# Contracting the second pass of the context logits over 104 rows in place of 64

## The chip, the cores and the metric

The kernel runs on one core of a Trainium2 chip. The metric is the device time of one execution in microseconds. Three timed runs of the kernel before gave 1978.53, 1979.91 and 1981.23 us; their median, 1979.91 us, is the time to be compared with.

## The reference

A network of four layers works on 1024 tokens (a grid of 16 rows and 64 columns) of 1024 features, with 256 further context tokens. Each layer norms its input, scales and shifts it, applies a mixer and adds the result to the stream. The mixers are pooling, neighbourhood attention, short convolution, and pooling again. The change lies in the attention, layer 1, which has 16 heads of 64 features. Each query sees keys in a window of the grid, with a bias, and all 256 context keys:

```python
s_ctx = jnp.einsum('brqhd,bchd->bhrqc', q, kc).astype(jnp.float32)
logits = jnp.concatenate([s_loc.reshape(...), s_ctx], axis=-1)
p = jax.nn.softmax(logits, axis=-1).astype(v.dtype)
```

All is float32.

## The kernel before

Activations lie transposed, features on partitions. A float32 value is held as two parts, hi + lo, each of which TensorE takes in one pass, and a product is hi*hi + hi*lo + lo*hi. The large projections do this in three matmuls per feature tile (`mm3`, L115 to L117).

In the attention (`na_attend`) the tokens stand in 8 blocks of 8 grid columns, 128 queries each, so there are 16 heads x 8 blocks = 128 steps. A head has 64 features, which is half of the 128 rows that a matmul can contract over. The logits use this: the first pass contracts over 128 rows, with the query's hi and lo part stacked (64 + 64) against the key's hi part twice. The second pass has the query's hi part (64 rows) against the key's lo part (64 rows). For the keys of the grid the second pass carries 40 more rows (`MROWS`): one-hot rows of the query's place against rows of 0 or -1e30 that mask the window. So for the grid's keys (PSUM tile `S`) it contracts over `KK` = 64 + 40 = 104 rows (L1153), and for the 256 context keys (tile `SC`), which need no mask, over 64 (L1155). In all four products the queries are the loaded weights and the keys are streamed.

One step of the loop is, in TensorE's order: for every second step the values of a pair of blocks (`O`, L1234 and L1235, alternately with the hi and the lo part of the probabilities); the transposes of one block's probabilities (`T`, and `TB` for a fifth chunk, L1209); about two and a half items of dense work (the projections of the next heads, later a share of the output projection); and the four products of the logits of the block three steps ahead (L1152 to L1155). Between them VectorE takes the maximum of the logits (L1167 for `SC`, L1169 for `S`), ScalarE the exponential (L1179), GpSimd multiplies by the reciprocal of the sum (`normalise`, L1188), and after the transposes ScalarE and VectorE split the result in hi and lo (`pthi` L1213, `ptlo` L1218). `S`, `SC`, `O` and `TB` have one buffer each, `T` has two.

The order on each engine is the order in which the program is written, and each engine runs its own in turn. `load_keys` issues the loads of a head's keys and values, one head ahead, on SyncE's queue. GpSimd's other work in this stretch is the lo part of weights (`wlo`, L80) and a gating product per pair of heads (L1244).

Of the kernel before, what the change touches and what calls it, by code (L numbers as in the profile page):

```python
"""Hybrid pool / neighbourhood-attention / short-conv backbone on one core.

Activations live transposed: features on partitions, tokens along the free axis.  A float32
product x*w is carried by three passes of the tensor engine over exact parts: x = xh + xl,
w = wh + wl (each part fits the engine's single-pass operand), xh*wh + xl*wh + xh*wl.
"""
# [10 lines left out]
F32 = mybir.dt.float32  # L17
# [7 lines left out]
P = 128  # L25
# [16 lines left out]
# columns of the packed per-feature vectors  # L42
# [4 lines left out]
class Tiles(list):  # L47
    """feature tiles of a chunk of tokens, and the pairs of them that share a slot"""
# [5 lines left out]
class Net:  # L54
# [8 lines left out]
    # ---------------------------------------------------------------- storage  # L63
# [6 lines left out]
    # chunks of tokens: halves, the two parts of the second half, the context  # L70
# [5 lines left out]
    # ---------------------------------------------------------------- pieces  # L76
    def split(self, hi, lo, src, lo_engine=None):
        """src (float32) = hi + lo"""
        self.nc.scalar.activation(hi, src, AF.Copy)  # L79
        (lo_engine or self.nc.vector).tensor_tensor(lo, src, hi.bitcast(F32), op=ALU.subtract)  # L80
# [15 lines left out]
    def weight_later(self, src, c0=0, c1=1024, lo_engine=None):  # L96
        """a weight whose parts are split by the steps that come with it"""
        raw = self.pw.tile([P, 1024], F32, tag="raw", name=self.nm("raw"), bufs=3)
        self.nc.sync.dma_start(raw[:, c0:c1], src[:, c0:c1])
        hi = self.pw.tile([P, 1024], F32R, tag="whi", name=self.nm("whi"))  # L100
        lo = self.pw.tile([P, 1024], F32R, tag="wlo", name=self.nm("wlo"))

        def step(c):
            s = slice(c, min(c + 256, c1))
            self.split(hi[:, s], lo[:, s], raw[:, s], lo_engine)
        return (hi, lo), [lambda c=c: step(c) for c in range(c0, c1, 256)]

    def mm3(self, ps, w, h, ks, begin=True, end=True):
        """ps (+)= sum over ks of w(k)^T h(k), both operands as pairs of parts"""
        t = self.nc.tensor  # L110
        ks = list(ks)
        for k in ks:
            wh, wl = w(k)
            hh, hl = h(k)
            t.matmul(ps, wh, hh, start=(begin and k == ks[0]), stop=False)  # L115
            t.matmul(ps, wh, hl, start=False, stop=False)  # L116
            t.matmul(ps, wl, hh, start=False, stop=(end and k == ks[-1]))  # L117

    def ahead(self, fetch, args):
        """fetch(*a) for a in args, one ahead of its use"""  # L120
# [20 lines left out]
    # Short dependent products are traced a few long ones after their operands, so that the  # L141
    # tensor engine, which runs in this order, does not wait for them.
# [13 lines left out]
    # ---------------------------------------------------------------- modulation  # L156
    def ada_tile(self, l, conds, j, raw=None):
        """column j (128 features) of silu(cond) @ ada_w[l] + ada_b[l]"""
# [11 lines left out]
    def gain(self, l, c, k0=0, k1=KT):  # L170
        """A = norm_g * (1 + scale)"""
# [5 lines left out]
    def ada_all(self, l, x_parts, c_parts=()):  # L177
        """the modulation of a layer, one tile at a time"""
# [12 lines left out]
    def background(self, n=None):  # L191
        """modulation of later layers, between the weights of this one"""
# [15 lines left out]
    # ---------------------------------------------------------------- rms norm  # L208
# [7 lines left out]
    def sumsq_add(self, st, x, k, engine=None, whole=True):  # L216
        """the squares are summed here, the last one optionally by the product that sums partitions"""
# [12 lines left out]
    def rstd_tokens(self, st):  # L230
        """1/sqrt(mean square + eps), tokens on partitions"""
# [42 lines left out]
    def rstd_spread(self, dg, n):  # L274
        """the same on all partitions, tokens along the free axis (PSUM)"""
# [5 lines left out]
    def norm_later(self, xs, st, l, c, n, h, key, delays=(1, 2)):  # L281
        """h[key] = parts of the modulated norm of xs, traced behind the next products"""
# [16 lines left out]
    def modulate_k(self, x, rs, l, c, k, hi, lo, n, pool=None, act=False):  # L299
        """(hi, lo) parts of x * rstd * A + B for one feature tile"""  # L300
# [12 lines left out]
    def hparts(self, n=HALF):  # L313
        """fresh (hi, lo) tiles for the 8 feature tiles of one chunk of tokens"""
# [26 lines left out]
    # ---------------------------------------------------------------- out projection  # L341
    def out_proj(self, wsrc, y, l, groups, xold, spill, order=range(KT), ks={}):
        """x_new[k] (per chunk) = xold + gate * (y @ w_out); sums of squares on the way.  The chunks of a
        group share their weights.  `ks` may
        restrict the sum of a chunk's tile to some feature tiles, with the others' share in xold."""
# [31 lines left out]
    # ---------------------------------------------------------------- pooling mixer  # L377
    POOL_ORDER = (6, 7, 4, 5, 2, 3, 0, 1)

    def pool_in(self, li, h, chunks, start=None):  # L380
        """y (float32) per feature tile: {k: {ch: AP}}; `start` may make the first products itself"""
# [6 lines left out]
        def put(t, ch, ps=None):  # L388
# [19 lines left out]
            if ch == "c":  # L408
                dst = y[k][ch] if kind == "g" else Uc[k][:, 16:16 + CTX]
                # the products of the shifts  # L410
# [22 lines left out]
        def mix(gi, ch, Wg):  # L433
# [12 lines left out]
            for j, k in enumerate(ks):  # L446
                u = Uc[k] if ch == "c" else U[k]
                # sum over the window [t - w/2, t + w/2) by doubling
# [10 lines left out]
                # windows cut by an end of the sequence hold fewer tokens  # L459
# [21 lines left out]
        # products that do not wait for the second half of the tokens come first  # L481
# [20 lines left out]
        for t in todo:  # L502
# [9 lines left out]
            # the mixing products of the group before, now that their operands are there  # L512
# [11 lines left out]
    # ---------------------------------------------------------------- layers  # L524
# [28 lines left out]
    def consts(self):  # L553
# [12 lines left out]
        # the conditions on all partitions  # L566
# [8 lines left out]
        # per layer and kind of token: gain, (shift, scale, gate)  # L575
# [6 lines left out]
    def squares(self, x):  # L582
        """sum of the squares of a half's tokens, but for the sum over partitions"""
# [14 lines left out]
    def load_pair(self, xs, src, k, off):  # L598
        """feature tiles k and k + 1, which share a slot"""
# [3 lines left out]
    def scratch(self):  # L603
# [5 lines left out]
        # keys of pairs, values of fours of heads  # L609
# [15 lines left out]
    def layer0(self):  # L625
# [7 lines left out]
        # out tokens by halves of the grid's columns  # L633
# [16 lines left out]
    def start(self, h, put, shift, W):  # L650
        """the norms of layer 0 and the first products.  A half's products are those of x * A, as the
        modulation of each feature tile arrives; 1/rms of the tokens and the products of the shift,
        which go along with the context's as one more token, come to them afterwards."""
# [19 lines left out]
        def block(t):  # L673
            """the weights of a tile, which lie in blocks of P columns ordered by k, then tile"""
# [7 lines left out]
        # the order in which the operands are needed  # L682
# [11 lines left out]
        def high(ch, x, k):  # L694
            """(hi, lo) parts of x * A"""
# [31 lines left out]
        def square(ch, x, j):  # L727
            """the squares of a pair of tiles are summed"""
# [73 lines left out]
        def gained_c(k):  # L802
            """the same for the context, the shifts of both kinds of tokens as two more tokens"""
# [78 lines left out]
    # ---------------------------------------------------------------- neighbourhood attention  # L882
    def store_kq(self, part, hp, ch, ps):
        """parts of a pair's keys or scaled queries to DRAM"""
# [21 lines left out]
    def kq_steps(self, pairs, h, early=None):  # L906
        """the projections of pairs' keys and queries, a few matrix products at a time; `early`
        is stepped along once the last pair is done with the first half of the tokens"""
# [34 lines left out]
    def mask_rows(self):  # L943
        """constant rows of the attention operands, rounded to their type"""
# [8 lines left out]
    def na_first(self, h):  # L953
        """values and gates of all heads, keys and queries of the first pair"""
# [51 lines left out]
    def y_rows(self, y, p):  # L1006
        """parts of half p of the grid's rows, from tokens in column-block order"""
# [11 lines left out]
    def x1_rows(self, ch, k):  # L1019
        """half of the rows of the residual, from tokens in column-block order"""  # L1020
# [8 lines left out]
    def out_ahead(self):  # L1029
        """operands of out_steps"""  # L1030
# [17 lines left out]
    def out_steps(self):  # L1048
        """the first heads' share of the output's first half (and of a little more), while the
        last heads attend"""  # L1050
# [28 lines left out]
    def load_keys(self, h):  # L1079
# [11 lines left out]
        ld(KC[0:HD, CTX:2 * CTX], self.dkc[hp][1, r])  # L1091
        dv = self.dv[h // 4][:, :, h % 4]
# [13 lines left out]
    def na_attend(self, hx):  # L1106
        """returns y (float32, tokens in column-block order) per feature tile"""
# [26 lines left out]
        def logits(n):  # L1134
# [20 lines left out]
            nc.tensor.matmul(SC[:], Q[0:HD, 1, q0], KC[0:HD, CTX:2 * CTX], start=False, stop=True)  # L1155
            tiles[n] = (S, SC)

        def maximum(n):
# [6 lines left out]
            # negated logits and their minimum  # L1165
# [24 lines left out]
        def transpose(n):  # L1190
# [4 lines left out]
            # chunk order: key blocks up to 2mp+1, context, then (odd b) block 2mp+2  # L1195
# [54 lines left out]
        # stores are issued once their data are there, so that the loads behind them do not wait  # L1250
# [151 lines left out]
def _edges():  # L1402
    e = np.ones((P, 4, 16), np.float32)
    for gi in range(4):
# [3 lines left out]
        for j in range(w // 2 - 1):  # L1408
            # tokens L - (w/2 - 1) + j
# [29 lines left out]
def _ntiles(w, cols=P):  # L1439
    """[K, N] -> [N/cols, 128, K/128 * cols]: per tile of output features, contiguous per partition"""  # L1440
# [4 lines left out]
def _interleave(w, tiles):  # L1445
    """chosen tiles of _ntiles, their blocks of P columns ordered by k, then tile"""
# [4 lines left out]
def _feat(a):  # L1451
    """[..., F] -> [128, ... * F/128]"""
# [4 lines left out]
def _blocks(xT):  # L1457
    """row-major grid tokens -> column blocks of 8"""
# [4 lines left out]
def _bias(rpb):  # L1463
    """[16, 15, 31] -> [16, 128 queries (r, c), 3 * 128 keys (block offset, r', c')], zero outside the table"""
# [48 lines left out]
```

## Time and profile before

| what | value |
|---|---|
| timed runs, median (lowest to highest) | 1979.91 us (1978.53 to 1981.23) |
| span of the profiled execution | 1977.3 us |
| device time of that execution | not listed apart from its span |
| PE (matmul) busy | 1902.4 us, 96% |
| PEld (weight load) busy | 1607.0 us, 81% |
| DVE, ACT, POOL busy | 1103.4, 727.7, 565.1 us |
| chain that ended last, by engine | PE 77%, DVE 12%, DMA 5% |
| chain, by line: L1155 | 2% |

PE is TensorE's matmuls and PEld its weight loads, which can run beside a matmul. DVE is VectorE, ACT ScalarE, POOL GpSimd and SPq the queue of SyncE, which issues the DMAs. The spans of matmuls are modelled at their ends, and matmuls overlap in the pipeline: how fast TensorE goes through them is read from the distance of their starts, not from their lengths.

### The profile page before, as it was taken

To read this page: it belongs to the slowest core of one execution; us is meant where nothing else is said; L and a number is where in the kernel's file an instruction comes from. 1 tells how busy PE (TensorE), PEld (TensorE's weight loads), DVE (VectorE), ACT (ScalarE), POOL (GpSimd) and SP (SyncE) were. 2 spreads that over 40 slices of the span, in tenths; PEclk is the share of its full clock that TensorE was granted. 3 is DMA by queue.
4 is the path that set the end of the run, shared out by engine and by line. 5 is a ranking of instruction groups with operands and counts; after the bars stand their busy time and mean duration, and the time that the engine had idled before them with its cause. 6 is when DMAs were issued, how large, how long until landed. Compare 5 with 4: busy or idle time off the path is not lost.

```text
span 1977.3 us, 27078 instructions
## 1 busy us (share of the span) xinstructions
PE 1902.4 (96%) x9936; PEld 1607.0 (81%) x9936; DVE 1103.4 (56%) x2251; ACT 727.7 (37%) x1401; POOL 565.1 (29%) x536
## 2 busy tenths in 40 slices
PE   7789889999999999999999999999999999999997
PEld 4677778889988888888887787788888887888887
DVE  7989986346521066666666668744222246532536
ACT  3432225344122255555555656321122135322322
POOL 4545323552110133333333434100000023333120
PEclk9899999999999999999999999999999999999999
DMA  6232362554863456566568637534111155011234
GB/s 248 75 112 91 116 193 59 192 165 136 277 200 107 157 160 180 178 191 180 159 185 233 194 107 232 173 113 132 45 52 48 48 181 171 16 49 48 67 123 152
DMA packets 126960, 274.21 MB, mean 139 GB/s; under 512 B 12874, under 2 KB 48458, under 8 KB 126828
## 3 DMA queue, kind: packets, MB, share of 16 engines
q1 hardware_dynamic: 126828, 272.49, 44.3%
q8 instruction: 78, 1.28, 0.3%
q14 instruction: 54, 0.44, 0.1%
HBM read 218.63 MB, written 53.81 MB: 138 GB/s over the span
## 4 chain that ended last, share of the span: by engine, by line
PE 77%; DVE 12%; DMA 5%; issue 3%; POOL 2%; ACT 1%; SPq 0%; DVEq 0%; POOLq 0%; ACTq 0%
PE mm L115 21%; PE mm L117 21%; PE mm L116 21%; DVE junk L166 4%; PE T L1209 3%; PE O L1234 3%; PE O L1235 2%; PE SC L1155 2%; DMA raw<-in_ada 2%; PE S L1152 1%; DMA a<-x 1%; PE S L1153 1%; DVE S L455 1%; POOL S L455 1%; DMA a<-in_xT 1%
## 5 line engine op out<-in xcount | busy, mean ns | idle before, releaser
L115 PE MATMUL mm<-a,whi 128*128 128x512 f32 (+2 forms) x2160 | 820.2, 380 | 23.5 <-DVE U L418 11.1
L117 PE MATMUL mm<-a,wlo 128*128 128x512 f32 (+2 forms) x2160 | 806.5, 373 | 5.0 <-POOL wlo L80 3.3
L116 PE MATMUL mm<-a,whi 128*128 128x512 f32 (+2 forms) x2149 | 802.8, 374 | 7.4 <-DVE a L80 6.6
L115 PEld LDWEIGHTS mm<-a,whi 128*128 128x128 f32 x2160 | 410.6, 190 | 95.6 <-DVE U L418 12.4
L117 PEld LDWEIGHTS mm<-a,wlo 128*128 128x128 f32 x2160 | 409.6, 190 | 79.7 <-POOL wlo L80 4.8
L116 PEld LDWEIGHTS mm<-a,whi 128*128 128x128 f32 x2149 | 408.7, 190 | 76.6 <-DVE a L80 8.4
L79 ACT ACTIVATE whi<-raw 128x1024 fp32r<-128x1024 f32 (+2 forms) x237 | 170.8, 738 | 356.2 <-PE mm L116 273.3
L80 POOL TENSOR_TENSOR wlo<-raw,whi 128x256 fp32r<-128x256 f32 (+2 forms) x150 | 190.0, 1280 | 386.8 <-ACT whi L79 359.8
L1188 POOL TENSOR_SCALAR pr<-pr,rsum 128x640 f32<-128x640 f32 (+1 forms) x128 | 99.1, 774 | 277.3 <-DVE rsum L1187 252.5
L166 DVE CUSTOM_DVE_ANT_0 junk<-raw,sil_x,vec 128x1024 bf16<-128x1024 f32 x86 | 120.3, 1399 | 91.7 <-DMA raw<-in_ada 91.4
L80 DVE TENSOR_TENSOR wlo<-raw,whi 128x1024 fp32r<-128x1024 f32 (+1 forms) x87 | 108.1, 1243 | 112.2 <-ACT whi L79 111.2
L115 PE MATMUL mm<-a,a 128*128 128x512 f32 (+2 forms) x280 | 98.0, 350 | 8.6 <-ACT a L698 7.4
L1167 DVE TENSOR_SCALAR_CACHE_REDUCE lg<-SC 128x256 f32<-128x256 f32 x128 | 54.3, 424 | 92.8 <-PE SC L1155 92.3
L1179 ACT ACTIVATE pr<-lg,nmx 128x640 f32<-128x640 f32 (+1 forms) x128 | 102.2, 799 | 1.9 <-DVE nmx L1169 1.9
L224 POOL TENSOR_TENSOR a<-a,a 128x512 f32<-128x512 f32 x42 | 59.9, 1427 | 142.0 <-ACT a L223 133.2
L116 PE MATMUL mm<-a,a 128*128 128x512 f32 (+2 forms) x275 | 96.1, 350 | 3.8 <-DVE a L702 3.0
L117 PE MATMUL mm<-a,a 128*128 128x512 f32 (+2 forms) x280 | 97.0, 346 | 0.5 <-DVE a L80 0.5
L1218 DVE TENSOR_TENSOR ptlo<-T,pthi 128x512 fp32r<-128x512 f32 x128 | 88.5, 692 | 14.8 <-ACT pthi L1213 10.9
L1234 PE MATMUL O<-pthi,a 128*128 128x256 f32 x352 | 93.5, 301 | 1.1 <-ACT pthi L1213 1.1
L1235 PE MATMUL O<-ptlo,a 128*128 128x256 f32 x352 | 87.4, 284 | 0.6 <-DVE ptlo L1218 0.6
L1213 ACT ACTIVATE pthi<-T 128x512 fp32r<-128x512 f32 x128 | 76.3, 596 | 25.5 <-PE T L1209 24.5
L1209 PE MATMUL T<-ident,pr 128*128 128x128 f32 x512 | 78.2, 276 | 0.0
(181 smaller groups left out, 2501.5 us busy)
## 6 DMA issues: line engine op xcount, KB each, us to landing
raw<-in_ada SPq DMA_DIRECT2D x86, 512.0 KB
raw<-in_pool_out SPq DMA_DIRECT2D x32, 512.0 KB
raw<-in_conv_in SPq DMA_DIRECT2D x32, 512.0 KB
raw<-in_pool_in SPq DMA_DIRECT2D x27, 512.0 KB
x<-a SPq DMA_DIRECT2D x48, 256.0 KB
raw<-in_na_in SPq DMA_DIRECT2D x24, 512.0 KB
a<-dk SPq DMA_DIRECT2D x48, 256.0 KB
dv<-v SPq DMA_DIRECT2D x40, 256.0 KB
```

Source lines behind the costliest of these rows:

```text
L79: self.nc.scalar.activation(hi, src, AF.Copy)
L80: (lo_engine or self.nc.vector).tensor_tensor(lo, src, hi.bitcast(F32), op=ALU.subtract)
L115: t.matmul(ps, wh, hh, start=(begin and k == ks[0]), stop=False)
L116: t.matmul(ps, wh, hl, start=False, stop=False)
L117: t.matmul(ps, wl, hh, start=False, stop=(end and k == ks[-1]))
L166: nc.vector.tensor_tensor_reduce(out=junk[:], in0=raw[:], in1=self.sil[c][:], scale=1.0, scalar=self.vec[:, b:b + 1], op0=ALU.mult, op1=AL ...
L1179: nc.scalar.activation(pr[:, :L + CTX], lg[:, :L + CTX], AF.Exp, bias=nm[:], scale=-1.0, accum_out=sm[:])
L1188: nc.gpsimd.tensor_scalar(pr[:, :L], pr[:, :L], rs[:], 1.0, op0=ALU.mult, op1=ALU.mult)
L1209: nc.tensor.transpose(T[:, (s - b0) * P:(s - b0 + 1) * P], pr[:, o:o + P], self.ident[:])
L1218: nc.vector.tensor_tensor(lv, tv, hv.bitcast(F32), op=ALU.subtract)
L1234: nc.tensor.matmul(ops[:], v, hi[:, s, :], start=(n == 0), stop=False)
L1235: nc.tensor.matmul(ops[:], v, lo[:, s, :], start=False, stop=(n == len(seq) - 1))
```

## The change

`load_keys` sets 40 rows of zeros under the lo part of a head's context keys, and the second pass of `SC` contracts over 104 rows. On the query's side these rows hold the one-hot rows that are there for L1153, so the 40 rows add nothing to the sums.

```diff
@@ load_keys
         ld(KC[0:HD, CTX:2 * CTX], self.dkc[hp][1, r])
+        self.nc.gpsimd.memset(KC[HD:HD + MROWS, CTX:2 * CTX].bitcast(F32), 0.0)
         dv = self.dv[h // 4][:, :, h % 4]
@@ logits
             nc.tensor.matmul(SC[:], Q[:, 0, q0], KC[:, 0:CTX], start=True, stop=False)
-            nc.tensor.matmul(SC[:], Q[0:HD, 1, q0], KC[0:HD, CTX:2 * CTX], start=False, stop=True)
+            nc.tensor.matmul(SC[:], Q[0:KK, 1, q0], KC[0:KK, CTX:2 * CTX], start=False, stop=True)
```

The rest of the diff takes comments away. The instructions of PE, DVE, ACT and SP stand in the same order as before, with waits for the same engines and queues. GpSimd has 16 memsets more, one for each head, each in the place where the head's loads are written. This is GpSimd's order around the load of head 3 (`pr` probabilities, `wlo` the lo part of a weight, `a` the buffer of the context keys; lines after the change are two higher). Before:

```order
L1188 TENSOR_SCALAR pr_6819<-pr_6819,rsum_6833 128x640 [waits DVE_49,PE_49]
L80 TENSOR_TENSOR wlo_6803<-raw_6800,whi_6802 128x256 [waits Activation_49] x2
L1188 TENSOR_SCALAR pr_6857<-pr_6857,rsum_6887 128x640 [waits DVE_49,PE_49]
L1188 TENSOR_SCALAR pr_6925<-pr_6925,rsum_6943 128x640 [waits DVE_49,PE_49]
L1188 TENSOR_SCALAR pr_6966<-pr_6966,rsum_6980 128x640 [waits DVE_49,PE_49]
```

And the same place in the changed kernel:

```order
L1190 TENSOR_SCALAR pr_6822<-pr_6822,rsum_6836 128x640 [waits DVE_49,PE_49]
L80 TENSOR_TENSOR wlo_6806<-raw_6803,whi_6805 128x256 [waits Activation_49] x2
L1093 MEMSET a_6865 40x256 [waits DMAHW4_49,DMAHW1_49,Pool_49]
L1190 TENSOR_SCALAR pr_6860<-pr_6860,rsum_6891 128x640 [waits DVE_49,PE_49,Pool_49]
L1190 TENSOR_SCALAR pr_6929<-pr_6929,rsum_6947 128x640 [waits DVE_49,PE_49]
L1190 TENSOR_SCALAR pr_6970<-pr_6970,rsum_6984 128x640 [waits DVE_49,PE_49]
```

The memset stands between two pieces of a weight and a `normalise`, and waits for two DMA queues: for the transfers of the buffer's earlier tenants, here two stores of keys.

## Rows read from the trace of the kernel before

**Rows 1.** Windows, attention: us; busy of PE, PEld, DVE, ACT, POOL; clock; DMA share; GB/s.

```profile
685.00:1165.00 480.00, 474.00 (x2757) 398.28 (x2756) 306.85 (x976) 273.82 (x674) 171.48 (x214) 0.99 0.63 182
```

**Rows 2.** Groups, shapes apart, 685 to 1165 us: busy us, mean ns | idle before.

```profile
L1155 PE MATMUL SC<-a,a 64*128 64x256 f32 x128 | 49.2, 384 | 0.0
L1154 PE MATMUL SC<-a,a 128*128 128x256 f32 x128 | 36.3, 283 | 0.0
...
L1155 PEld LDWEIGHTS SC<-a,a 64*128 64x128 f32 x128 | 23.6, 184 | 23.0 <-issue 18.6
...
L1153 PE MATMUL S<-a,a 104*128 104x256 f32 x32 | 9.2, 287 | 0.5 <-DMA a<-dmask 0.5
```

**Rows 3.** Timeline of PE and PEld, logits, then values: start us, length us.

```profile
792.66 0.19 PEld L1153 LDWEIGHTS S<-a,a 104*128 104x128 f32 x1
792.84 0.34 PE L1153 MATMUL S<-a,a 104*128 104x384 f32 x1
...
793.01 0.28 PE L1154 MATMUL SC<-a,a 128*128 128x256 f32 x1
793.23 0.18 PEld L1155 LDWEIGHTS SC<-a,a 64*128 64x128 f32 x1 [0.20 <-issue]
793.23 0.38 PE L1155 MATMUL SC<-a,a 64*128 64x256 f32 x1
793.53 0.19 PEld L1234 LDWEIGHTS O<-pthi,a 128*128 128x128 f32 x1
793.54 0.38 PE L1234 MATMUL O<-pthi,a 128*128 128x256 f32 x1
...
793.76 0.28 PE L1235 MATMUL O<-ptlo,a 128*128 128x256 f32 x1
...
793.88 0.28 PE L1234 MATMUL O<-pthi,a 128*128 128x256 f32 x1
```

**Rows 4.** Timeline, transposes behind values, then behind the logits; a `normalise` between.

```profile
728.47 0.27 PE L1209 MATMUL TB<-ident,pr 128*128 128x128 f32 x1
...
728.58 0.60 PE L1209 MATMUL T<-ident,pr 128*128 128x128 f32 x4
728.62 0.80 POOL L1188 TENSOR_SCALAR pr<-pr,rsum 128x640 f32<-128x640 f32 x1 [2.07 <-DVE rsum L1187]
...
731.64 0.38 PE L1155 MATMUL SC<-a,a 64*128 64x256 f32 x1
...
731.95 0.33 PE L1209 MATMUL TB<-ident,pr 128*128 128x128 f32 x1
...
732.12 0.60 PE L1209 MATMUL T<-ident,pr 128*128 128x128 f32 x4
```

**Rows 5.** Timeline, the tightest meeting of the lo part and the values.

```profile
799.94 0.69 DVE L1218 TENSOR_TENSOR ptlo<-T,pthi 128x512 fp32r<-128x512 f32 x1 [0.16 <-ACT pthi L1213]
...
800.75 0.33 PE L1235 MATMUL O<-ptlo,a 128*128 128x256 f32 x1
```

**Rows 6.** Timeline, the tightest meeting of the maximum and the next logits.

```profile
746.99 0.08 DVE L1169 DVE_READ_ACCUMULATOR2_ANT nmx<- 128x1 f32 x1
...
747.13 0.44 PE L1152 MATMUL S<-a,a 128*128 128x384 f32 x1
```

**Rows 7.** Groups of the whole span: a memset on POOL.

```profile
L1113 POOL MEMSET pthi<- 128x128 f32 x1 | 0.2, 205 | 0.0
```

**Rows 8.** Timeline of SP's queue, a store of keys: start us, length of the issue.

```profile
742.54 0.38 SPq L899 DMA_DIRECT2D dk<-a  x1
```

**Rows 9.** Timeline of POOL at the place shown in the change.

```profile
755.12 1.43 POOL L80 TENSOR_TENSOR wlo<-raw,whi 128x256 fp32r<-128x256 f32 x2
756.74 0.80 POOL L1188 TENSOR_SCALAR pr<-pr,rsum 128x640 f32<-128x640 f32 x1 [0.19 <-DVE rsum L1187]
```

**Rows 10.** Windows, where the dense work changes to the output's share.

```profile
1045.00:1125.00 80.00, 74.28 (x397) 60.31 (x395) 52.16 (x151) 47.00 (x115) 30.94 (x38) 0.96 0.79 220
```

**Rows 11.** The chain of waits in that stretch: its longest piece.

```profile
1076.25 8.49 DMA a<-x
```

## The prediction

> **What bounds the kernel now.** I read the page first: PE is busy 96% of the span and holds 77% of the chain that ended last, so a product is worth its time wherever PE never rests. The windows come next, for the stretch in which the changed product runs: from 685 to 1165 us PE is busy 474.0 of 480 us, the granted clock is 0.99 of full speed (2.4 GHz), and DVE (306.9), ACT (273.8) and POOL (171.5) are far from full [rows 1]. What TensorE saves there is saved from the end, as long as nothing else comes late.
>
> Then the groups of that stretch with shapes kept apart. The second pass for the context keys (L1155, 64 rows) lasts 384 ns in the mean, the first pass of the same size (L1154, 128 rows) 283 ns, and the second pass for the grid's keys, where it streams as many columns (L1153, 104 rows), 287 ns [rows 2]. So the shortest contraction is the longest product, and 104 rows cost what 128 cost. The weight loads of L1155 have 23.0 us of idle time before them, 18.6 of it waiting for nothing that the profile shows [rows 2].
>
> The timeline tells where this comes from [rows 3]. A load normally runs beside the product before its own: L1153's load starts at 792.66 and its product at 792.84. L1155's load starts at 793.23, with its own product, and so does the load of the product behind it (793.53 against 793.54). So TensorE goes from one product to the next without overlap twice, on the way from 128 rows to 64 and on the way back. Starts of 256-column products normally stand 0.12 us apart (793.76 to 793.88). Here the distances are 0.22 (793.01 to 793.23), 0.31 (to 793.54) and 0.22 (to 793.76). L1153, with 104 rows, shows none of this on either side: with 384 columns in it the product behind it starts 0.17 us later (792.84 to 793.01).
>
> The Trainium skill has a rule for this: in "TensorEngine Tiling (Array Packing)", section Tiling Modes, it says that changing the tiling mode drains TensorE. Rows 3 agree for 64 against 128 rows, and by that rule a product of 104 rows, which fits no 64-row tile, needs no change of mode.
>
> **The change part by part.** *The product.* It stands 128 times. In half of the steps the values follow (rows 3), in the other half the transposes (rows 4); at the loop's start two are followed by dense work, which I count as values.
> - Before values: (0.22 - 0.12) + (0.31 - 0.12) + (0.22 - 0.12) = 0.39 us each; 64 x 0.39 = 25.0 us.
> - Before transposes: 0.10 in front and 0.31 - 0.12 = 0.19 behind (731.64 to 731.95), as above. The transpose after that stands 0.17 us off (731.95 to 732.12), where it is 0.11 when values come first (728.47 to 728.58): 0.06 more [rows 4]. 64 x 0.35 = 22.4 us.
>
> Together 47 us, if the product with 104 rows behaves as L1153 does. No more columns are streamed and no instruction is added on PE, so nothing stands against it there.
>
> *What comes late next.* With TensorE faster, three meetings become tighter.
> - The lo part of the probabilities and the values. Between transposes and values stand dense work and the logits; the logits lose 0.10 + 0.19 = 0.29 us there. In the tightest of each eight pairs of blocks `ptlo` ends at 800.63 and the product that reads it starts at 800.75 [rows 5]: 0.12 us of slack, so 0.17 us of waiting, in 8 pairs: 1.4 us. The others have more than 0.29.
> - The maximum and the next logits, since `S` has one buffer. In the tightest of each sixteen steps the maximum ends at 747.07 and L1152 starts at 747.13 [rows 6]; it waits already. From L1155's end to that point TensorE becomes about 0.2 us faster (0.19 and 0.06 to 0.10 behind it, less the 0.10 by which it is itself shorter). 8 x 0.2 = 1.6 us.
> - The DMAs. From 1045 to 1125 us they are busy 0.79 of the time and PE idles 80 - 74.3 = 5.7 us, with the clock at 0.96 [rows 10]; one load of the residual takes 8.49 us there [rows 11]. This stretch has no room to gain its share. If it cannot shrink at all, 47 x 80 / 480 = 8 us of the gain are lost; if the loads fall better, its 5.7 us can go. I take a loss of 2, nearer to the rows as they stand.
>
> *The memsets.* The trace has no memset of 40 x 256. One of 128 x 128 takes 205 ns [rows 7]; twice the columns make at most 410, so each costs 0.2 to 0.4 us and all 16 at most 6.6 us, on POOL. What hides them: POOL is busy 171.5 of 480 us [rows 1], and a `normalise` that ends at 729.42 feeds transposes that start at 731.95, 2.5 us later [rows 4]. Without that cover the 16 would cost 3 to 7 us. I count nothing. Behind each memset on POOL stand a `normalise` and pieces of weights. Its waits are for old transfers: the store of keys in the place shown was issued at 742.54, and POOL comes there at 756.55, 14 us later [rows 8, 9], longer than the longest landing of rows 11. The waits of the other engines are as before.
>
> **The sum.** The span of 1977.3 us less 47, plus 1.4 + 1.6 for the waits and 2 for the DMAs, is 1935.3 us. The median of the runs stands 2.6 us above the span (1979.9 - 1977.3); with that, 1938 us.
>
> **The rivals.**
> 1. *No change.* The long product is slow for another reason (its buffer, its operand), or 104 rows are split as 64 are. Then nothing is saved and the memsets are hidden: 1980 us. For it speaks that "issue" names no cause [rows 2]; against it, that the disturbance begins with the load of L1155 and is undone behind the next product, and that L1153, with the same queries and 104 rows, shows none [rows 3]. The Trainium skill has a sentence on this side: "TensorE: Matmul & The Clock Gate", section Why this matters for your kernels, says that one matmul with K = 32 takes the same time as one with K = 128. By that, rows filled up would give nothing; rows 2 disagree for 64 rows (384 ns against 283).
> 2. *Half of it comes back.* TensorE goes as fast as computed, but the pipeline around it does not follow. A step takes 480 / 128 = 3.75 us and would take 3.4; DVE needs 306.9 / 128 = 2.4, ACT 2.1, the DMAs 0.63 x 3.75 = 2.4 us of each [rows 1], so none of them becomes the bound on the whole. It would have to come from meetings: all 64 pairs wait 0.17 us (11 us), the stretch of rows 10 gains nothing (8), and the maximum costs 1.6 more than I took (3 in all): 22 us of 47 are given back, 1955 us. Against it: most pairs have slack left.
> 3. *Slower.* The memset holds POOL's queue, because it waits for a transfer, and the `normalise` behind it, and with it the transposes, come late. A hold of h us costs 16 x (h - 2.5); it eats the whole gain from h = 47 / 16 + 2.5 = 5.4 us on. With the 8.49 us of rows 11 for each it costs 16 x 6 = 96 us: 1980 - 47 + 96 = 2029 us. For it speaks that the memset does wait for DMA queues; against it the 14 us of rows 8 and 9.
>
> **How the numbers follow.** My forecast has a chance of 0.84, with its own spread: without any of the losses, and with the 5.7 us of rows 10 gone too, 1980 - 47 - 6 = 1927 us; with the 8 us lost there and waits twice as long, 1947. Rival 1 has 0.04, rival 2 0.10, rival 3 0.02. The range reaches from 1928, the better end, to 1951, most of the way to rival 2, and leaves out about 0.15. About 0.2% (4 us) is what a measurement here can tell from no change. Faster than that are the forecast and rival 2: 0.94; the same, rival 1: 0.04; slower, rival 3: 0.02.
>
> **What would show it.** In the profile of the changed kernel the second pass for the context keys has a mean of about 285 ns, its load starts one product ahead, and the idle time before its loads is nearly gone. The starts around it stand 0.12 us apart, and the second transpose 0.11. The stretch of rows 1 becomes some 42 us shorter than its 480; what lies before and behind it stays. PE's waits for `ptlo` and for the maximum grow to about 3 us. The forecast is wrong if the load still starts with its own product (rival 1), if PE's idle time in the attention rises from 6 to over 20 us (rival 2), or if POOL idles before the memsets (rival 3).

## The result, and the profile after

The changed kernel took 1943.78 us (median of 4 runs, 1940.08 to 1948.25) against 1979.34 us before in the same session: 35.6 us less, a ratio of 0.9822 with an interval of 0.9801 to 0.9843. The forecast was 1938 us, with a range of 1928 to 1951. All ratios here compare fast executions alone; two slow ones (2111 us with the memsets alone, 4728 with 65 rows) are left out of them. The profiled execution has a span of 1942.1 us against 1977.3.

The changed product, all occurrences (lines are two higher than before: L1157 answers to L1155):

```profile
L1157 PEld LDWEIGHTS SC<-a,a x128: 189/190/336, 684.8 to 1127.3; 104*128 104x128 f32 x128
L1157 PE MATMUL SC<-a,a x128: 281/285/419, 684.9 to 1127.4; 104*128 104x256 f32 x128
```

Its median is 285 ns (mean 287), where the mean was 384 [rows 2], and there is no "issue" idle time before it any more. The timeline of logits followed by values, the answer to [rows 3] (start us, length us):

```profile
782.43 0.34 PE L1155 MATMUL S<-a,a 104*128 104x384 f32 x1
...
782.60 0.28 PE L1156 MATMUL SC<-a,a 128*128 128x256 f32 x1
782.61 0.19 PEld L1157 LDWEIGHTS SC<-a,a 104*128 104x128 f32 x1
782.72 0.29 PE L1157 MATMUL SC<-a,a 104*128 104x256 f32 x1
782.72 0.19 PEld L1236 LDWEIGHTS O<-pthi,a 128*128 128x128 f32 x1
782.84 0.29 PE L1236 MATMUL O<-pthi,a 128*128 128x256 f32 x1
...
782.96 0.28 PE L1237 MATMUL O<-ptlo,a 128*128 128x256 f32 x1
```

The load of the second pass starts with the product ahead of it (782.61 against 782.60), and the starts stand 0.12 us apart throughout. The attention as a whole, in windows with the columns of [rows 1]; the second row answers to [rows 10]:

```profile
685.00:1129.00 444.00, 433.31 (x2749) 393.00 (x2749) 302.28 (x976) 274.06 (x673) 176.92 (x229) 0.99 0.67 196
```

```profile
1010.00:1090.00 80.00, 70.62 (x402) 61.83 (x401) 51.69 (x153) 48.00 (x117) 33.62 (x42) 0.94 0.77 222
```

The stretch has become 36 us shorter than the 480 of before. PE idles 10.7 us in it where it idled 6.0, and 9.4 of these lie between 1010 and 1090 us, where the dense work changes to the output's share. PE's waits there (us in total, times, longest):

```profile
PE O L1236 <- ACT pthi L1215: 3.2, 1, 3.2
PE S L1154 <- DVE nmx L1171: 2.3, 2, 2.1
PE S L1154 <- DMA a<-dq: 2.1, 1, 2.1
```

I read what the change gave from the starts of the first product of the logits (L1152 before, L1154 after). From step to step the distance is 0.38 us shorter where values follow and 0.33 where transposes follow: 64 x 0.38 + 64 x 0.33 = 45.4 us, if nothing comes late. Up to step 96 the loop gained 30.3 us (347.4 us before, 317.1 after) of 96 x 0.355 = 34.1, and over the last 31 steps 4.6 (130.0, 125.4) of 11.0. So 3.8 us are missing in the steady part and 6.4 in the last quarter. The first logits start 0.9 us earlier (684.6 against 685.5), and what follows the last ones takes 0.6 us longer (815.0 against 814.4).

### The profile page after: what moved, and what is told of

It is laid out like the page before. It is cut to its first block, busy times and chain, and to the rows that moved or that the text cites. A ratio compares the mean times of both kernels' runs of the same rounds, so it can differ in the third digit from the quotient of the medians.

```text
span 1942.1 us, 27112 instructions
## 1 busy us (share of the span) xinstructions
PE 1864.4 (96%) x9936; PEld 1604.0 (83%) x9936; DVE 1095.8 (56%) x2251; ACT 729.1 (38%) x1401; POOL 571.1 (29%) x552
## 4 chain that ended last, share of the span: by engine, by line
PE 76%; DVE 12%; DMA 6%; issue 3%; POOL 2%; ACT 1%; SPq 0%; DVEq 0%; POOLq 0%; ACTq 0%
PE mm L117 22%; PE mm L115 21%; PE mm L116 21%; DVE junk L166 4%; PE T L1211 3%; PE O L1237 2%; PE O L1236 2%; DMA raw<-in_ada 2%; PE S L1154 1%; DVE S L455 1%; PE S L1155 1%; POOL S L455 1%; DMA a<-in_xT 1%; PE SC L1157 1%; PE SC L1156 1%
## 5 line engine op out<-in xcount | busy, mean ns | idle before, releaser
L79 ACT ACTIVATE whi<-raw 128x1024 fp32r<-128x1024 f32 (+2 forms) x237 | 170.9, 738 | 352.1 <-PE mm L116 273.6
L1236 PE MATMUL O<-pthi,a 128*128 128x256 f32 x352 | 89.0, 286 | 3.2 <-ACT pthi L1215 3.2
```

Source lines behind the costliest of these rows:

```text
L1236: nc.tensor.matmul(ops[:], v, hi[:, s, :], start=(n == 0), stop=False)
```

## The experiments

**The memsets alone.** Before, plus:

```diff
+        self.nc.gpsimd.memset(KC[HD:HD + MROWS, CTX:2 * CTX].bitcast(F32), 0.0)
```

> The kernel before with one part of the change alone: the 16 memsets of 40 x 256 zeros, while the second pass of the context logits keeps its 64 rows. My theory (all of the gain is in the product, the memsets are hidden): 1979 us, within 2 of before. Rival (the memsets cost what they last, 16 x 0.31 us): 1984 us.

Measured: 1978.49 us, ratio 0.9998 (0.9986 to 1.001). The memsets cost nothing that can be measured. The group of the 16 in its trace (count; min/median/max ns; first and last start in us):

```profile
L1092 POOL MEMSET a<- x16: 307/308/311, 570.0 to 1118.1; 40x256 f32 x16
```

**One row more than 64.**

```diff
+        self.nc.gpsimd.memset(KC[HD:HD + 1, CTX:2 * CTX].bitcast(F32), 0.0)
-            nc.tensor.matmul(SC[:], Q[0:HD, 1, q0], KC[0:HD, CTX:2 * CTX], start=False, stop=True)
+            nc.tensor.matmul(SC[:], Q[0:HD + 1, 1, q0], KC[0:HD + 1, CTX:2 * CTX], start=False, stop=True)
```

> The second pass of the context logits contracts over 65 rows, 64 plus a single row of zeros, in place of 64 (before) or 104 (changed). Theory (what costs is the change between products that fit 64 rows and products that do not): 1944 us, as with 104 rows. Rival (the product becomes cheaper with each row of it, 35.6 us for 40 rows): 1978 us.

Measured: 1942.82 us, ratio 0.9814 (0.9796 to 0.9832), the same as with 104 rows. The product with 65 rows:

```profile
L1156 PE MATMUL SC<-a,a x128: 279/285/288, 684.4 to 1124.8; 65*128 65x256 f32 x128
```

It lasts 285 ns like the one with 104. Between 64 and 65 rows lies the whole difference; the rival of a graded cost falls.

**Two products of 64 rows, adjacent and apart.** Both start from the kernel before, with the two products of `SC` first. `C2a` and `C2b` are the second pass over columns 0 to 127 and 128 to 255, `S1` and `S2` the products of the grid's keys.

```diff
-            S1; S2; C1; C2
+            C1; C2a; C2b; S1; S2        # adjacent
+            C1; C2a; S1; C2b; S2        # apart
```

> 64 rows as before, but the 256 columns of that pass are done by two products of 128 columns that stand next to each other; both products of the context logits stand ahead of the two of the grid's keys. One change of row count on the way in and one on the way out in each step, as before. Theory: before plus at most 0.1 us for each of the 128 additional products, 1979 to 1992 us. Rival (each 64-row product is slow by itself, by 0.3 us): 1979 + 128 x 0.3 = 2017 us.

> As the run with two adjacent products of 128 columns, but with the first product of the grid's keys (128 rows) between them, so that the row count changes four times in a step in place of two. Theory: the adjacent run plus 128 x 0.34 to 0.39 us, 44 to 50 us more, 2023 to 2042 us. Rival (slow by itself): the same time as the adjacent run.

Measured: adjacent 1986.19 us (ratio 1.0038, 1.0025 to 1.0051), apart 2024.9 us (1.0227, 1.0207 to 1.0248). The same products with the same columns cost 38.7 us more when they stand apart. Timeline of the adjacent ones:

```profile
799.80 0.28 PE L1152 MATMUL SC<-a,a 128*128 128x256 f32 x1
800.01 0.18 PEld L1153 LDWEIGHTS SC<-a,a 64*128 64x128 f32 x1 [0.24 <-issue]
800.01 0.32 PE L1153 MATMUL SC<-a,a 64*128 64x128 f32 x1
800.11 0.19 PEld L1154 LDWEIGHTS SC<-a,a 64*128 64x128 f32 x1
800.17 0.27 PE L1154 MATMUL SC<-a,a 64*128 64x128 f32 x1
800.37 0.19 PEld L1155 LDWEIGHTS S<-a,a 128*128 128x128 f32 x1
800.38 0.39 PE L1155 MATMUL S<-a,a 128*128 128x256 f32 x1
```

And of those apart:

```profile
803.96 0.28 PE L1152 MATMUL SC<-a,a 128*128 128x256 f32 x1
804.17 0.18 PEld L1153 LDWEIGHTS SC<-a,a 64*128 64x128 f32 x1 [0.25 <-issue]
804.17 0.32 PE L1153 MATMUL SC<-a,a 64*128 64x128 f32 x1
804.42 0.19 PEld L1154 LDWEIGHTS S<-a,a 128*128 128x128 f32 x1
804.42 0.44 PE L1154 MATMUL S<-a,a 128*128 128x384 f32 x1
804.80 0.18 PEld L1155 LDWEIGHTS SC<-a,a 64*128 64x128 f32 x1 [0.19 <-issue]
804.80 0.33 PE L1155 MATMUL SC<-a,a 64*128 64x128 f32 x1
805.05 0.19 PEld L1156 LDWEIGHTS S<-a,a 104*128 104x128 f32 x1
805.05 0.45 PE L1156 MATMUL S<-a,a 104*128 104x384 f32 x1
```

Of two adjacent 64-row products the second one's load starts at 800.11, ahead of its product at 800.17: between equals the load runs beside the product. Apart, each of the four changes of row count has a load that starts with its own product (804.17, 804.42, 804.80, 805.05). What costs is the change, and a product of 64 rows is not slow by itself. The size, 38.7 / 128 = 0.30 us for the second pair of changes, is below the 0.34 to 0.39 I expected. In the traces of the two runs one step differs by 0.34 us (median), the low end of that; the rest is missing in the last quarter, where the 31 steps differ by 7.4 us in place of 10.4. Why is not shown.

**Where the rest of the gain stayed: the steady part.** The changed kernel ran again beside the next three, with 1944.58 us.

> The changed kernel once more, beside the runs of this call: 1944 us.

```diff
-            fill(rate)
-            fill(rate)
+            for _ in range(2):
+                fill(rate + (0.375 if n % 2 else -0.375))
```

> The changed kernel, with the dense work between the attention's steps spread otherwise: 3.25 items in a step whose next step begins with the values, 1.75 in the other, in place of 2.5 in each. In the trace of the changed kernel the two tight meetings (the lo part of the probabilities and the values; the maximum and the next logits) cost about 0.53 us in each 16 steps, both behind a step of the first kind. Theory: this gives them more lead, and up to 4.3 us come back: 1940 us. Rival (the waits move to the other steps, or the late part of the attention is what counts): 1944 us or more.

Measured: 1941.07 us, ratio 0.981 (0.9796 to 0.9823), 3.5 us less than the changed kernel beside it. The tight place of [rows 5], first the transposes that stand ahead of it in the kernel before, then transposes and values in the changed kernel:

```profile
798.61 0.60 PE L1209 MATMUL T<-ident,pr 128*128 128x128 f32 x4
```

```profile
787.50 0.60 PE L1211 MATMUL T<-ident,pr 128*128 128x128 f32 x4
...
788.82 0.69 DVE L1220 TENSOR_TENSOR ptlo<-T,pthi 128x512 fp32r<-128x512 f32 x1
...
789.18 0.28 PE L1236 MATMUL O<-pthi,a 128*128 128x256 f32 x1
789.57 0.19 PEld L1237 LDWEIGHTS O<-ptlo,a 128*128 128x128 f32 x1 [0.31 <-DVE ptlo L1220]
789.57 0.38 PE L1237 MATMUL O<-ptlo,a 128*128 128x256 f32 x1
```

The product waits for `ptlo`, which ends at 789.51, and starts 0.39 us behind the one ahead of it in place of 0.12. With the dense work spread by parity the loop up to step 96 takes 313.8 us in place of 317.1: of the 3.8 us that are missing in the steady part 3.2 come back. The intervals of the two runs overlap a little (this one ends at 0.9823, the changed one beside it spans 0.9811 to 0.9841), so that the gain is shown by the trace rather than by the times.

**The last quarter: lighter loads.** `x1_rows` and `y_load` load columns 0 to 511 alone, and `x1_rows` and `y_rows` use them for both halves:

```diff
-        self.nc.sync.dma_start(t[:], self.x1[k])
+        self.nc.sync.dma_start(t[:, 0:HALF], self.x1[k][:, 0:HALF])
...
-        self.nc.sync.dma_start(t[:], self.dy[k][:])
+        self.nc.sync.dma_start(t[:, 0:HALF], self.dy[k][:, 0:HALF])
```

> The kernel before with lighter loads in the late part of the attention: of the residual and of the first heads' results only the first 512 of 1024 columns are loaded, and used for both halves of the rows (this part of the computation is changed). 12 + 6 loads become 256 KB in place of 512 KB there. Base for the next run: 1979 us, or up to 6 less if the 5.7 us of idle time there go.

> The changed kernel with the same lighter loads (the same part of the computation changed). The product alone gives 45.8 us in the starts of the changed trace, the tight meetings take 4, and some 6 more are lost after 1000 us. Theory (these 6 are lost to transfers that do not become faster with TensorE): with lighter loads the change gains 40 to 42 us over its base. Rival (they are lost on ACT, DVE or POOL, or by the clock): 35 to 36 us, as with full loads.

Measured: 1974.80 us (ratio 0.9982, 0.9973 to 0.9991) and 1939.18 us (0.9801, 0.9785 to 0.9817). The change gains 35.6 us over its base, as with full loads, so that my theory falls as I had put it: fewer bytes speed up both kernels, by 4.2 and 5.4 us, and do not give the missing part back. That does not mean that no transfer comes late: ACT still waits for the residual, 9.5 us in 5 waits with the change (14.0 in 6 with full loads) and 6.3 in 4 without (13.6 in 5).

**The last quarter: who is held by the loads.** In the changed kernel ScalarE copies each loaded residual (L1026) and waits for it in its own order. One such load in the chain of waits (start us, length us), and ScalarE's timeline behind it:

```profile
1068.27 7.74 DMA a<-x
```

```profile
1076.03 0.63 ACT L1026 ACTIVATE a<-a 128x512 f32<-128x512 f32 x1 [4.80 <-DMA a<-x]
1076.57 1.01 ACT L79 ACTIVATE whi<-raw 128x256 fp32r<-128x256 f32 x3
1077.49 0.71 ACT L1181 ACTIVATE pr<-lg,nmx 128x512 f32<-128x512 f32 x1
1078.10 0.19 ACT L1181 ACTIVATION_READ_ACCUMULATOR pr<-lg,nmx 128x1 f32 x1
1078.19 0.58 ACT L1215 ACTIVATE pthi<-T 128x512 fp32r<-128x512 f32 x1
```

`pthi`, which PE waits for (3.2 us in the waits above), stands behind a copy that waited 4.80 us, a load that took 7.74 us, and the pieces of work that had gathered. The next loads are held there too. From 1068 to 1080 us SyncE's queue waits for the lo part of a weight, to have its buffer free, and GpSimd, which makes the lo part, waits for the hi part (`whi`, L79), which stands behind the copy (us in total, times, longest):

```profile
SPq L99 <- POOL wlo L80: 7.8, 1, 7.8
```

```profile
POOL wlo L80 <- ACT whi L79: 6.4, 1, 6.4
```

Two edits go at this, from two sides, and a third run joins them with the spread by parity. The copy later (`x1_load` and `x1_copy` are the two halves of `x1_rows`):

```diff
-            old = self.x1_rows(ch, n)
+            late = self.x1_load(n)
             for k in self.EARLY:
+                if k == self.EARLY[-2]:
+                    old = self.x1_copy(late, ch)
```

The loads of keys and queries earlier:

```diff
-            if b == 4 and h + 1 < HEADS:
+            if b == 3 and h + 1 < HEADS:
                 load(h + 1)
-            if b == 5 and h + 1 < HEADS:
+            if b == 4 and h + 1 < HEADS:
                 load_q(h + 1, 0)
```

> The changed kernel, with the loads of the next head's keys and of its first queries each written one step earlier. At head 13 this puts the queries ahead of two loads of the first heads' results (512 KB each) in SyncE's queue. In the trace of the changed kernel the logits of that head's first block wait 2.05 + 0.41 us for these queries, and the clock falls to half for 3.4 us. Theory (that wait is a transfer that comes late): it goes, 2.5 to 4 us faster than the changed kernel, 1941 us. Rival (the buffers are not free earlier, so that SyncE waits in its queue and other loads come late): 1944 us or more.

> The changed kernel, with ScalarE's copy of the loaded residual written behind the fourth of six feature tiles of an output's share, and its load where it was. In the trace of the changed kernel ScalarE waits in this copy for its load (14.0 us in 6 waits), and with it the splits of the probabilities behind it; TensorE then idles 2.1 us at 1056 and 3.2 + 0.3 us at 1079, with two stretches of 3.4 us at half clock. Theory: these waits go, 5 to 9 us faster than the changed kernel, 1935 to 1939 us. Rival (TensorE waits there for other transfers, the heads' keys and queries): 1943 to 1946 us.

> The kernel before with the same late copy of the residual. Its own idle times there are 2.3 us at 1089 and 1.1 + 0.3 us at 1112, with one stretch of 6.8 us at half clock. Theory: 4 to 7 us faster than before, 1972 to 1975 us, and the change is then worth about 38 us (this run less the changed kernel with the late copy). Rival: 1979 us.

> The changed kernel with all three: dense work spread by parity, the loads of keys and queries one step earlier, and the late copy of the residual. Theory (the three take away different waits): 3.5 + 3 + 6 us less than the changed kernel, 1932 us. Rival (they take away the same waits, or one brings a new one): 1937 to 1941 us.

| run | us | ratio to before (interval) |
|---|---|---|
| loads earlier, changed | 1953.10 | 0.987 (0.9857 to 0.9884) |
| copy later, changed | 1934.03 | 0.9774 (0.9758 to 0.9791) |
| copy later, before | 1972.76 | 0.9969 (0.9956 to 0.9981) |
| all three, changed | 1936.48 | 0.978 (0.9764 to 0.9796) |

The late copy takes 9.8 us off the changed kernel, a little more than I had put at most, and 6.2 off the one before (1979.0 us beside these runs). ACT's wait for the residual and the same window as above, with the copy later:

```profile
ACT a L1028 <- DMA a<-x: 1.2, 1, 1.2
```

```profile
1010.00:1090.00 80.00, 76.71 (x473) 68.05 (x473) 60.09 (x181) 55.44 (x136) 38.26 (x48) 1.00 0.85 252
```

14.0 us of waiting in 6 times have become 1.2 in one; PE idles 3.3 us there in place of 9.4, the granted clock stays at full speed, and the DMAs move 252 GB/s in place of 222. So the transfers could go faster. That they were late because what waits for them also holds what asks for the next is shown at the one place above; for the others it is not shown.

The earlier loads made it worse, and the time is on their rival's side; that the buffers were not free earlier is not shown. The wait for the queries went, and another came. PE's and ACT's longest waits in that run:

```profile
PE S L1154 <- DVE nmx L1171: 13.0, 3, 9.6
```

```profile
ACT a L1026 <- DMA a<-x: 22.0, 5, 10.6
```

The residuals came later, and PE waited 9.6 us in one piece for DVE behind them. All three together were not better than the late copy alone. The late copy with the spread by parity and without the earlier loads was not run.

With the late copy on both sides the change is worth 1972.76 - 1934.03 = 38.7 us, 3.1 more than without. Each of these times is known to about 3 us, so this difference is not settled by the times. The traces say more. In the pair with the late copy the loop's last 31 steps take 123.6 and 113.4 us, 10.2 us gained of 11.0 in place of 4.6, and neither has a stretch at half clock in the attention. But the 6.4 us that were missing lie in two places, and the late copy can have given back only one of them. 3.1 us are lost in the two steps around 1032 us, where PE waits for queries; the first copy of a residual stands behind them, at 1039 us. The other 3.4 us are lost in the steps from there on, and with the late copy on both sides these lose 0.9. The trace with the late copy loses nothing at the queries either, but it is one execution, the fastest of its four; every other trace of a kernel with 65 or 104 rows loses there, the second one of the changed kernel too (5.1 us).

## Why the prediction was right, point by point

*The product.* Foretold 0.39 and 0.35 us per step, 47.4 in all; the starts show 0.38 and 0.33, 45.4. The mechanism is shown by the runs with 65 rows and with two products apart. Rival 1 is out. The sentence of the Trainium skill that the prediction set beside it ("TensorE: Matmul & The Clock Gate", section Why this matters for your kernels) speaks of K = 32, which no run here has; for 64 rows between products of 128 it doesn't carry over, as one row of zeros more took 36 us off the kernel.

*The tight meetings.* Foretold 1.4 us for the lo part and 1.6 for the maximum, at the two places where they came. The first cost more than I worked out: per 16 steps it takes the whole 0.38 us of a step, where I had 0.17. Two things were wrong in the working. I let the product that reads `ptlo` come 0.29 us earlier, but it is the second product of the values and so loses the 0.10 behind the first one as well, 0.39 in all. And I took all of the 0.12 us as slack, while in the changed trace the product starts 0.06 us behind the end of `ptlo` (789.51 to 789.57) and waits. 0.39 - 0.06 is 0.33; the rest goes in the distances next to it. `ptlo` itself did not come later: it ends 2.0 us behind the start of the transposes in both traces (798.61 to 800.63 and 787.50 to 789.51). The second meeting took about 0.15 of 0.2. Each of the two comes five times in the first 96 steps, which makes 2.7 of the 3.8 us that are missing there; the others are in the first three steps (0.6) and in steps 89 to 92 (0.4). I had 3.0 for both in all 128 steps.

*The DMAs.* This is the term that was mis-sized: foretold a loss of 2 us between 0 and 8, measured 6.4 over the last 31 steps. I had named the stretch and put its lateness down to the transfers. For half of it that may stand: 3.1 us are lost in the two steps where PE waits 2.1 us for queries and then goes at half clock. No run isolates this place: with the loads earlier the wait for the queries was gone, but the same two steps lost 3.3 us, while ScalarE waited 4.4 us for the first heads' results. What holds PE there stays open. For the other 3.4 us the runs showed something else. Half the bytes did not give them back, but the late copy did, down to 0.9: what counts is the place of the copy in ScalarE's line, where it holds the split of the probabilities for PE (3.2 us at 1079). ScalarE does not wait longer for the residual than before (13.6 us in 5 waits before, 14.0 in 6 after); PE loses more by it. PE's waits at the same three places in the kernel before, to be set beside the 3.2, 2.1 (of 2.3) and 2.1 us of after:

```profile
PE O L1234 <- ACT pthi L1213: 1.1, 1, 1.1
PE S L1152 <- DVE nmx L1169: 2.3, 1, 2.3
PE S L1152 <- DMA a<-dq: 0.4, 1, 0.4
```

In the changed kernel each of the three is followed by a stretch of 3.4 us at half clock (1.2 GHz), from 1032, 1056 and 1080 us on; in the 4 us ahead of them PE was busy for 1.9, 1.9 and 0.8 us. The kernel before has one such stretch of 6.8 us. The window that begins with the second:

```profile
1056.00:1060.00 4.00, 4.00 (x15) 3.36 (x15) 3.93 (x9) 3.95 (x10) 1.54 (x2) 0.57 1.07 282
```

By the same miss the stretch of [rows 1] became 36 us shorter and not the 42 that I had named as a sign.

*The memsets.* Foretold 0.2 to 0.4 us each and hidden; they take 0.31 us and the run with them alone is at 0.9998. In the changed kernel POOL starts each of them 0.06 us behind the instruction ahead of it, so that it does not wait for the transfers. Rival 3 is out.

*Rival 2* foretold 1955 us by waits in all pairs. PE's idle time rose from 6.0 to 10.7 us, not over 20, and 7 of 8 pairs do not wait.

*The sum.* Foretold were 42.0 us less in the span, measured 35.2. Of the 6.8 us between them 1.6 are the product's, 0.8 the steady part's and 4.4 the last quarter's, all on the same side. That the forecast missed by 5.8 us and not by more is luck: I added 2.6 us for the distance of the median from the profiled span, and in the changed kernel this is 1.7.

## What to carry to other kernels

Where products of 64 rows stand singly among products of more, look at the starts of their weight loads. A load that starts with its own product, on the way in and on the way out, costs time (0.33 to 0.38 us for each such product here), and rows of zeros, even a single one, take it away. After such a gain on the busiest engine, look for engines that wait for a load in their own order and hold something that the busy engine needs. Writing the consumer of the load later was worth 9.8 us here; writing other loads earlier, those of keys and queries, cost 9. Asking for the residual itself earlier was not tried.

## What was not expected

One row of zeros does as well as 40. A product of 64 rows and 128 columns next to its equal starts 0.16 us behind it, later than the 0.12 us at which products of 128 rows and 256 columns follow each other. And the load that was moved one step ahead made its kernel 9 us slower, and in that run the waits for another load, the residual, grew from 14.0 to 22.0 us.
